# Mixture of experts: from 128-row blocks shared by two experts in split arithmetic to 64 rows for each expert in plain fp32

## The chip, the cores and the metric

The kernel runs on one core of a Trainium2 chip. The metric is the device time of one execution in microseconds (us); the median of 3 runs of the kernel before is 3462.05 us (3460.3 to 3463.83). A core has five engines with instruction queues of their own: TensorE (PE; its weight loads are listed as PEld), VectorE (DVE), ScalarE (ACT), GpSimd (POOL) and SyncE (SP, which here only issues transfers), and 16 DMA engines that carry out the transfers.

## What is computed

Two transformer blocks run one after the other on 1024 tokens of 1024 values. The change concerns the last step of the second block, a mixture of 64 experts. A router picks for each token one of 8 groups and then the two best of its 8 experts. Each expert is a small gated network, and a token's two results are added with their gates:

```python
e_in_group = jnp.take_along_axis(e_logits, g_sel[:, None, None], axis=1)[:, 0]
top_p, top_j = lax.top_k(e_prob, TOP_K)                     # TOP_K = 2
gate = g_prob_of_group * top_p / jnp.sum(top_p, axis=-1, keepdims=True)
h = jax.nn.silu(xb @ w1[e]) * (xb @ w3[e])                  # xb: 1024 wide, h: 256 wide
y = h @ w2[e]                                               # 1024 wide
```

An expert has 1024x512 values in `w1` and `w3` together and 256x1024 in `w2`, 3 MB in fp32. All 64 experts are 192 MB, and every one of them is read once. The 2048 rows (1024 tokens, two experts each) give an expert 32 rows on average. With the reference's own inputs the fullest experts have 75, 69 and 64 rows, and the fullest pair (b, b + 32) has 115.

## The kernel before

The program runs its stages in order: the first block, the second block's mixers, the merge (`phase_merge`, which also computes the router's scores), the routing (`phase_route`) and the experts (`phase_moe`). Only the last three are touched.

**Blocks.** Experts b and b + 32 share a block of 128 slots. `phase_route` counts each token's place within its pair and writes three tables by a matmul with one-hot rows: `idx` (which token sits in a slot), and two columns of `gate`, one for each of the two experts, of which one is zero for every slot. Both experts of a block compute on all 128 rows; the gate cancels the rows of the other. A table for slots beyond 128 (`idxo`, `gateo`, `eid`) feeds a loop at the end (`For_i`, L2073), which runs as many times as there are such blocks.

**Arithmetic.** Matmuls are done in fp32r. To keep fp32 accuracy every operand is split in a high part (`nc.scalar.copy` to an F32R tile) and a low part (`nc.vector.tensor_tensor` subtract), and three products are added: high by high, high by low, low by high. `wsplit` (L2000) does it for each piece of the weights, `xT` (L1990) for the transposed tokens, `hT` (L2022) for the hidden values.

**Weights.** A piece is 512 KB (128 partitions of 4 KB). `rawload` (L1942) issues one on SP's queue into the next of 34 slots (`NR` = 19 on the right side of the memory, of which 16 hold the merge's `mt` tiles first and 3 stage its weights, and `NL` = 15 on the left). `prefetch` (L1951) issues pieces ahead: during the merge as `mt` tiles come free, 13 more in `phase_route`, 4 more from POOL at the start of `phase_moe`. From then on SP issues a piece when the split has read an old one. `rawload`'s queue is in program order, so a load that waits holds up those behind it.

**Order in `phase_moe`.** Expert by expert (L2053): transposes of the hidden values of the last expert, `up` of this expert (8 steps of 128 rows, three products each, into one PSUM bank), `down` of the last one into `py`; after the second expert of a block `py` is copied by ACT and added to `out` by an indirect DMA on POOL's queue (`scatter`, L1973). Tokens are fetched two blocks ahead by an indirect DMA (`gather`, L1968).

Of the kernel before, what the change touches and what calls it, by code (L numbers as in the profile page):

```python
# [8 lines left out]
F32 = mybir.dt.float32  # L9
F32R = mybir.dt.float32r  # L10
# [10 lines left out]
NR, NL, NB, PF = 19, 15, 30, 2  # L21


def layout(inp):
# [34 lines left out]
    def heads(a, b):  # L59
# [32 lines left out]
                                    .reshape(64, 8, 128, 512).transpose(0, 2, 1, 3))  # L92
# [27 lines left out]
class K:  # L120
# [1515 lines left out]
    def phase_merge(self):  # L1636
# [22 lines left out]
        self.Oe = rp.tile([128, 2, 8, 32], F32, name="Oe")  # L1659
        with ExitStack() as st:  # L1660
# [45 lines left out]
            with ExitStack() as s1:  # L1706
# [15 lines left out]
                for c in range(8):  # L1722
# [3 lines left out]
                    if c >= 1:  # L1726
                        self.prefetch(PF if c > 1 else NR - 14)
# [98 lines left out]
    def phase_route(self):  # L1826
# [11 lines left out]
        self.gate = rp.tile([128, 2, 32], F32, name="gate")  # L1838
        self.gateo = rp.tile([128, 2, 16], F32, name="gateo")
        self.eid = rp.tile([128, 17], I32, name="eid")  # L1840
        self.rawL = self.pool("rawL", NL, ctx=self.ctxm)
        self.prefetch(NB - self.npre)
        with ExitStack() as st:
# [4 lines left out]
            Og = self.O.rearrange("p h c (s g) j -> p h c s (g j)", s=2)  # L1848
            C32 = [128, 8, 32]
            Ob = p.tile(C32, BF16, name="Ob")  # L1850
            V.tensor_tensor(Ob, Oe[:, 0], Oe[:, 1], op=ALU.add)
# [3 lines left out]
            Pb = p.tile([128, 9, 32], BF16, name="Pb")  # L1855
            V.memset(Pb[:, 0, :], 0.0)
            for c in range(8):
                V.tensor_tensor(Pb[:, c + 1, :], Pb[:, c, :], Ob[:, c, :], op=ALU.add)
            pr = ps.tile(C32, F32, name="prk")
            nc.tensor.matmul(pr, usb[:, 0, :], Ob, start=True, stop=False)  # L1860
            nc.tensor.matmul(pr, usb[:, 1, :], Pb[:, 0:8, :], start=False, stop=True)
            W = p.tile([128, 2, 8, 3, 32], F32, name="W")
            for h in range(2):
                for v in range(3):
                    src = Oe[:, h] if v == 0 else Og[:, h, :, v - 1]
                    nc.gpsimd.tensor_tensor(W[:, h, :, v, :], src, val[:, :, h, min(v, 1), None].to_broadcast(C32), op=ALU.mult)
            rk = p.tile([128, 2, 8], F32, name="rnk")
            for h in range(2):
                J = p.tile(C32, F32, name=f"J{h}")
                V.tensor_tensor(J, Oe[:, h], pr, op=ALU.mult)  # L1870
                V.tensor_reduce(rk[:, h], J, axis=AX.X, op=ALU.add)
            pt = ps.tile([128, 3, 32], F32, name="ptab")
            for i in range(16):
                h, c = divmod(i, 8)
                q = p.tile([128, 128], F32, name="q1h", bufs=6)
                V.tensor_scalar(q, io, rk[:, h, c:c + 1], None, op0=ALU.is_equal)
# [3 lines left out]
            pc = ps.tile([128, 32], F32, name="pcn")  # L1880
            nc.tensor.matmul(pc, usb[:, 1, :], Pb[:, 8, :], start=True, stop=True)
            nb = p.tile([128, 32], F32, name="nb")
            V.tensor_scalar(nb, pc, 128.0, None, op0=ALU.is_gt)
            for b in range(2, 8):
                V.scalar_tensor_tensor(nb, pc, 128.0 * b, nb, op0=ALU.is_gt, op1=ALU.add)
            ci = p.tile([128, 32], F32, name="ci")
            V.tensor_tensor_scan(ci, self.ones[:, 0:32], nb, 0.0, op0=ALU.mult, op1=ALU.add)
            oe = p.tile([128, 32], F32, name="oe")
            V.tensor_sub(oe, ci, nb)
            ob = p.tile([128, 2, 8], F32, name="obk")  # L1890
            for h in range(2):
                J = p.tile(C32, F32, name=f"J{h}")
                V.tensor_tensor(J, Oe[:, h], oe[:, None, :].to_broadcast(C32), op=ALU.mult)
                V.tensor_reduce(ob[:, h], J, axis=AX.X, op=ALU.add)
            fl = p.tile([128, 2, 8], F32, name="fl")
            V.tensor_scalar(fl, rk, 128.0, None, op0=ALU.is_ge)
            for b in range(2, 8):
                V.scalar_tensor_tensor(fl, rk, 128.0 * b, fl, op0=ALU.is_ge, op1=ALU.add)
            rm = p.tile([128, 2, 8], F32, name="rm")
            V.scalar_tensor_tensor(rm, fl, -128.0, rk, op0=ALU.mult, op1=ALU.add)  # L1900
            V.scalar_tensor_tensor(ob, fl, -1.0, ob, op0=ALU.add, op1=ALU.add)
            mo = p.tile([128, 2, 8], F32, name="mo")
            V.tensor_scalar(mo, fl, 0.0, None, op0=ALU.is_gt)
            K16 = [128, 8, 16]
            Wo = p.tile([128, 2, 8, 3, 16], F32, name="Wo")
            for h in range(2):
                kq = p.tile(K16, F32, name=f"kq{h}")
                V.tensor_tensor(kq, io[:, None, 0:16].to_broadcast(K16), ob[:, h, :, None].to_broadcast(K16), op=ALU.is_equal)
                for v in range(3):
# [255 lines left out]
```

## Time and profile before

| | |
|---|---|
| median of 3 runs | 3462.05 us |
| span of the profiled execution | 3462.8 us |
| busy share over the span: PE, DVE, ACT, POOL | 94%, 68%, 46%, 14% |
| expert stage: first matmul to last, us from the start | 2856.5 to about 3443.5 |
| pieces of expert weights loaded | 384 of 512 KB (64 x 6) |

The shares over the whole span say little here, since the stages have different limits. From about 2857 us on only the experts run, and the rows below are read from that stretch, and from a few places elsewhere that show the price of an operation the stage doesn't have yet. In rows of matmuls the duration of one is its latency; matmuls are pipelined, and what they cost in a stream is the distance of their starts.

### The profile page before, as it was taken

The numbers are of one execution on the slowest core, as the hardware profiler recorded it, in microseconds if no ns is written. First come the engines' busy times: TensorE is split into PE (matmuls) and PEld (weight loads), VectorE is DVE, ScalarE is ACT, GpSimd is POOL, SyncE is SP. The second block draws the span as 40 slices with busy tenths as digits, with TensorE's granted clock in tenths as the row PEclk, the third lists the DMA queues.
The fourth block names the chain that finished last, engine by engine and source line by source line (L and its number), as shares of the span: only waits on it lengthen the run. The fifth ranks groups of instructions, "written<-read, shape, count | busy, mean of one in ns | idle before, by whom it ended". The sixth has DMA issues, their size and how long they took to land.

```text
span 3462.8 us, 45772 instructions
## 1 busy us (share of the span) xinstructions
PE 3265.8 (94%) x17125; PEld 2641.3 (76%) x17125; DVE 2364.0 (68%) x3850; ACT 1583.9 (46%) x2961; POOL 495.4 (14%) x342
## 2 busy tenths in 40 slices
PE   7999979976999999999999899999999979999997
PEld 3788868864788888888787787777787767777876
DVE  5754259989666565564778713468884568999997
ACT  4332235563432222222455412267763218888886
POOL 0000034454300000000333100000002011112110
PEclk9999989997999999999999999999999979999999
DMA  6722221043211111111211123110025559999994
GB/s 223 239 72 83 88 94 50 29 141 122 79 57 55 49 49 49 46 49 46 83 41 42 49 73 100 48 40 25 13 75 171 189 207 347 370 357 356 356 349 173
DMA packets 180656, 440.32 MB, mean 127 GB/s; under 512 B 22288, under 2 KB 73888, under 8 KB 180176
## 3 DMA queue, kind: packets, MB, share of 16 engines
q1 hardware_dynamic: 138160, 383.48, 31.7%
q10 hardware_dynamic: 31936, 32.54, 2.7%
q0 software_dynamic: 10336, 21.34, 2.4%
q8 instruction: 136, 2.23, 0.3%
q14 instruction: 88, 0.72, 0.1%
HBM read 396.39 MB, written 57.67 MB: 131 GB/s over the span
## 4 chain that ended last, share of the span: by engine, by line
PE 68%; DVE 13%; DMA 8%; ACT 5%; issue 4%; POOL 1%; SPq 0%; ACTq 0%; POOLq 0%; DVEq 0%
PE pj L222 8%; PE pd L1065 6%; PE ph L2015 5%; PE pg L910 5%; PE pg L908 5%; PE pg L906 5%; PE py L2037 3%; DMA wraw<-in_w_dram 3%; PE pw L945 2%; PE pmla L1685 2%; PE po L1741 2%; DMA wa<-in_wadaT_dram 1%; DVE y L1242 1%; DMA wraw<-in_w2e_dram 1%; PE po L1578 1%
## 5 line engine op out<-in xcount | busy, mean ns | idle before, releaser
L2005 DVE TENSOR_TENSOR wel<-wraw,weh 128x1024 fp32r<-128x1024 f32 x384 | 458.5, 1222 | 40.5 <-ACT weh L2004 35.5
L2004 ACT CAST weh<-wraw 128x1024 fp32r<-128x1024 f32 x384 | 391.0, 1055 | 83.2 <-PE ph L2015 80.6
L157 ACT CAST wh<-wf 128x1024 fp32r<-128x1024 f32 x136 | 142.6, 1049 | 593.0 <-PE pg L908 186.7
L158 DVE TENSOR_TENSOR wl<-wf,wh 128x1024 fp32r<-128x1024 f32 x104 | 129.1, 1241 | 208.5 <-ACT wh L157 207.8
L906 PE MATMUL pg<-hx,wh 128*128 128x512 f32 (+1 forms) x864 | 262.9, 384 | 8.5 <-DVE xt L1254 6.4
L908 PE MATMUL pg<-hx,wh 128*128 128x512 f32 (+1 forms) x864 | 261.8, 384 | 0.0
L910 PE MATMUL pg<-hx,wl 128*128 128x512 f32 (+1 forms) x864 | 261.7, 384 | 0.0
L1034 DVE SCALAR_TENSOR_TENSOR acc<-pad,fcw,acc 128x1024 f32<-128x1024 f32 x176 | 226.0, 1284 | 21.3 <-ACT acc L1031 16.8
L2015 PE MATMUL ph<-wel,xh 128*128 128x512 f32 x512 | 207.3, 405 | 6.4 <-DVE wel L2005 4.6
L2015 PE MATMUL ph<-weh,xh 128*128 128x512 f32 x512 | 206.4, 403 | 2.1 <-ACT weh L2004 2.1
L2015 PE MATMUL ph<-weh,xl 128*128 128x512 f32 x512 | 201.0, 393 | 0.0
L906 PEld LDWEIGHTS pg<-hx,wh 128*128 128x128 f32 x864 | 161.4, 190 | 41.6 <-ACT ainh L157 6.8
L910 PEld LDWEIGHTS pg<-hx,wl 128*128 128x128 f32 x864 | 161.4, 190 | 31.8 <-DVE wl L158 0.3
L908 PEld LDWEIGHTS pg<-hx,wh 128*128 128x128 f32 x864 | 161.5, 190 | 31.5
L1070 DVE SCALAR_TENSOR_TENSOR x<-pd,mod,x 128x1024 f32<-128x1024 f32 x42 | 53.8, 1282 | 136.3 <-PE pd L1065 136.3
L222 PE MATMUL pj<-hxh,wh 128*128 128x512 f32 x448 | 144.0, 398 | 0.0
L222 PE MATMUL pj<-hxl,wh 128*128 128x512 f32 x448 | 143.0, 398 | 0.0
L222 PE MATMUL pj<-hxh,wl 128*128 128x512 f32 x448 | 140.7, 395 | 0.0
L992 POOL TENSOR_TENSOR sx<-sx,sqx 128x1024 f32<-128x1024 f32 x7 | 20.4, 2918 | 723.1 <-ACT sqx L991 723.1
L2015 PEld LDWEIGHTS ph<-wel,xh 128*128 128x128 f32 x512 | 96.7, 189 | 32.3 <-DVE wel L2005 14.9
L157 ACT CAST wdh<-wdf 128x512 fp32r<-128x512 f32 (+1 forms) x44 | 25.6, 583 | 200.8 <-PE pd L1065 189.4
L1973 POOL DMA_INDIRECT out_dram<-yt,idx x32 | 50.5, 1577 | 464.6 <-ACT hh L2028 453.3
(683 smaller groups left out, 8337.9 us busy)
## 6 DMA issues: line engine op xcount, KB each, us to landing
wraw<-in_w_dram SPq DMA_DIRECT2D x252, 512.0 KB, 11.7
wraw<-in_w2e_dram SPq DMA_DIRECT2D x128, 512.0 KB, 12.0
wa<-in_wadaT_dram SPq DMA_DIRECT2D x32, 512.0 KB, 4.3
wf<-in_wconv_dram SPq DMA_DIRECT2D x28, 512.0 KB, 3.5
wf<-in_wgate_dram SPq DMA_DIRECT2D x22, 512.0 KB, 3.4
wf<-in_wup_dram SPq DMA_DIRECT2D x22, 512.0 KB, 3.4
wdf<-in_wdown_dram SPq DMA_DIRECT2D x40, 256.0 KB, 2.7
wst<-in_wada_dram SPq DMA_DIRECT2D x16, 512.0 KB, 10.2
```

Source lines behind the costliest of these rows:

```text
L157: nc.scalar.copy(hi, x)
L158: (eng or nc.vector).tensor_tensor(lo, x, hi.bitcast(F32), op=ALU.subtract)
L222: nc.tensor.matmul(ps[:, o:o + n], w[:, k, :], (hl if lo else hh)[:, k, ho:ho + n], start=k == 0 and i == 0, stop=k == 7 and i == 2)
L906: nc.tensor.matmul(ps[:, o:o + n], wh[:, k, :], xh[:, k, o:o + n], start=k == 0, stop=False)
L908: nc.tensor.matmul(ps[:, o:o + n], wh[:, k, :], xl[:, k, o:o + n], start=False, stop=False)
L910: self.lastmm = nc.tensor.matmul(ps[:, o:o + n], wl[:, k, :], xh[:, k, o:o + n], start=False, stop=k == nk - 1)
L1034: nc.vector.scalar_tensor_tensor(acc, pad[:, dy:dy + 16, dx:dx + 64], cw[:, f, tp:tp + 1], acc, op0=ALU.mult, op1=ALU.add)
L1065: nc.tensor.matmul(pp[:, o:o + 512], w[:, i, :], h[:, o:o + 512], start=i == 0 and w is wh and h is a, stop=i == n - 1 and w is wl)
L2004: nc.scalar.copy(h, f)
L2005: nc.vector.tensor_tensor(l, f, h.bitcast(F32), op=ALU.subtract)
L2015: nc.tensor.matmul(ph, a[:, k, :], b[:, j, :], start=k == 0 and a is xh and b is h, stop=k == 7 and a is xl)
L2037: nc.tensor.matmul(py[:, s * 512:s * 512 + 512], a[:, j, :], b[:, s, :], start=first and j == 0 and a is hh and b is h, stop=last and j == ...
```

## The change

- An expert gets 64 slots of its own: in a block, rows 0 to 63 belong to expert b, rows 64 to 127 to expert b + 32. `phase_route` counts places for 64 experts instead of 32 pairs; `gate` has one column.
- The matmuls of a block are plain fp32 (no F32R, no splits): for each step two matmuls, one for each expert, with a stationary operand of 64 columns, writing PSUM partitions 0 to 63 and 64 to 127 of the same bank, each with the weights of its own expert as the moving operand. `wsplit` and the second halves of `xT` and `hT` go away.
- A piece of weights is 1 MB (128 partitions of 8 KB), 6 for a block; `w13` is laid out on the host to make it contiguous. There are 18 slots (9 and 9), 8 of them shared with `mt`, one staging two (before: three) of the merge's weights.
- There are 33 blocks: 32 fixed ones and one for two experts with more than 64 rows, always run, whose expert numbers SP reads from `eid` at run time. Its results are added in two indirect DMAs, one for each half. The loop at the end runs if more is left over.
- Within a block the order is `up`, the transposes of the next block's tokens, `down`. `py` is copied half by ACT and half by DVE.

The loop's body changes in the same way and is left out below, as are the other lines of `overflow`.

```diff
-NR, NL, NB, PF = 19, 15, 30, 2
+NR, NL, NX = 9, 9, 33
...
     o["w13"] = np.ascontiguousarray(np.concatenate([f["exp_w1_2"][0], f["exp_w3_2"][0]], 2)
-                                    .reshape(64, 8, 128, 512).transpose(0, 2, 1, 3))
+                                    .reshape(64, 2, 4, 128, 512).transpose(0, 1, 3, 2, 4))
...
-        def mtile():
-            return self.rawR.tile([128, 2, 512], F32, name="wraw").rearrange("p a (b f) -> p (a b) f", b=4).bitcast(F32R)
-
-        stage = [self.rawR.tile([128, 2, 512], F32, name="wraw").rearrange("p a b -> p (a b)") for i in range(NR - 16)]
-        mt = [[mtile() for j in range(2)] for c in range(8)]
+        def slot():
+            return self.rawR.tile([128, 4, 512], F32, name="wraw")
+
+        stage = [t[:, 2 * j:2 * j + 2, :].rearrange("p a b -> p (a b)") for t in [slot() for i in range(NR - 8)] for j in range(2)]
+        mt = [[t[:, 2 * j:2 * j + 2, :].rearrange("p a (b f) -> p (a b) f", b=4).bitcast(F32R) for j in range(2)]
+              for t in [slot() for c in range(8)]]
...
-                        self.prefetch(PF if c > 1 else NR - 14)
+                        self.prefetch(1 if c > 1 else NR - 7)
...
-            Ob = p.tile(C32, BF16, name="Ob")
-            V.tensor_tensor(Ob, Oe[:, 0], Oe[:, 1], op=ALU.add)
+            O = self.O.rearrange("p h c g j -> p h c (g j)")
+            C64 = [128, 8, 64]
+            Ob = p.tile(C64, BF16, name="Ob")
+            V.tensor_tensor(Ob, O[:, 0], O[:, 1], op=ALU.add)
...
+            Pb = p.tile([128, 9, 64], BF16, name="Pb")
+            V.memset(Pb[:, 0, 0:32], 0.0)
+            V.memset(Pb[:, 0, 32:64], 8.0)
...
+            self.overflow(p, ps, rk, Pb, usb, O, io)
         self.ctxt.close()
...
+    def overflow(self, p, ps, rk, Pb, usb, O, io):
+        nc, V, val = self.nc, self.nc.vector, self.val
+        pc = ps.tile([128, 64], F32, name="pcn")
+        nc.tensor.matmul(pc, usb[:, 1, :], Pb[:, 8, :], start=True, stop=True)
+        nb = p.tile([128, 64], F32, name="nb")
+        for s in range(2):
+            self.floor(nb[:, 32 * s:32 * s + 32], pc[:, 32 * s:32 * s + 32], 1.0 / 64, 0.4921875 - 16.0 * s)
...
+        for i in range(16):
+            h, c = divmod(i, 8)
+            q = p.tile([128, 128], F32, name="q1h", bufs=6)
+            V.tensor_scalar(q, io, r[:, h, c:c + 1], None, op0=ALU.is_equal)
+            nc.tensor.matmul(pto, q, Wo[:, h, c], start=i == 0, stop=i == 15)
+        ix = self.table(p, pto, self.idxo, self.gateo, 16)
+        pm = p.tile([128, 2], F32, name="pm")
...
-    def rawload(self, src, key=None, eng=None):
-        P = self.rawR if self.nraw % (NR + NL) < NR else self.rawL
+        return ix
+
+    def rawload(self, src):
+        n = self.nraw % (NR + NL)
         self.nraw += 1
-        f = P.tile([128, 2, 512], F32, name="wraw")
-        (eng or self.nc.sync).dma_start(f, src)
-        if key is not None:
-            self.pre[key] = f
+        f = (self.rawR if n < NR else self.rawL).tile([128, 4, 512], F32, name="wraw")
+        self.nc.sync.dma_start(f, src)
         return f
 
-    def prefetch(self, num, eng=None):
-        T = self.T
+    def piece(self, q, e):
+        if q < 4:
+            return self.T["w13"][e[q % 2], q // 2]
+        return self.T["w2e"][e[q % 2]].rearrange("p a (b f) -> p (a b) f", b=2)
+
+    def prefetch(self, num):
         for n in range(self.npre, self.npre + num):
-            e, q = divmod(n, 6)
-            b, h = divmod(e, 2)
-            if q < 4:
-                self.rawload(T["w13"][b + 32 * h][:, 2 * q:2 * q + 2, :], ("u", e, q), eng)
-            else:
-                self.rawload(T["w2e"][b + 32 * h][:, q - 4, :].rearrange("p (a b) -> p a b", a=2), ("d", e, q - 4), eng)
+            b, q = divmod(n, 6)
+            self.pre[b, q] = self.rawload(self.piece(q, (b, b + 32)))
         self.npre += num
...
-            e.ph = self.pool(f"psH{b}", 1, PSUM, ctx=st)
-            e.px = self.pool(f"psX{b}", b, PSUM, ctx=st)
-            e.w = self.pool(f"ew{b}", 3 if b > 1 else 2, ctx=st, side="right")
+            e.ph = self.pool(f"psH{b}", b, PSUM, ctx=st)
+            e.px = self.pool(f"psX{b}", 1, PSUM, ctx=st)
...
+        HALF = [slice(64 * s, 64 * s + 64) for s in range(2)]
...
-            return xh, xl
-
-        def wsplit(P, src, key):
-            f = self.pre.pop(key, None) or self.rawload(src)
-            h = P.w.tile([128, 2, 512], F32R, name="weh")
-            l = P.w.tile([128, 2, 512], F32R, name="wel")
-            nc.scalar.copy(h, f)
-            nc.vector.tensor_tensor(l, f, h.bitcast(F32), op=ALU.subtract)
-            return h, l
-
-        def up(P, w, xh, xl, gate, e=None):
+            t = P.t.tile([128, 8, 128], F32, name="xTt")
+            nc.scalar.copy(t, pt)
+            return t
+
...
+        def up(P, w, x, gate):
             ph = P.ph.tile([128, 512], F32, name="ph")
-            for q in range(4):
-                h, l = wsplit(P, w[:, 2 * q:2 * q + 2, :], ("u", e, q))
-                for j in range(2):
-                    k = 2 * q + j
-                    for a, b in ((xh, h), (xh, l), (xl, h)):
-                        nc.tensor.matmul(ph, a[:, k, :], b[:, j, :], start=k == 0 and a is xh and b is h,
-                                         stop=k == 7 and a is xl)
+            for q in range(2):
+                f = w(2 * q), w(2 * q + 1)
+                for j in range(4):
+                    k = 4 * q + j
+                    for s, m in enumerate(HALF):
+                        nc.tensor.matmul(ph[m], x[:, k, m], f[s][:, j, :], start=k == 0, stop=k == 7)
...
-        def hT(P, s):
+        def down(P, w, s, ix, apart=None):
...
-        def down(P, w, py, hh, hl, first, last, e=None):
+            h = P.t.tile([128, 2, 128], F32, name="hT")
+            nc.vector.tensor_copy(h, pt)
+            py = P.py.tile([128, 1024], F32, name="py")
+            f = w(4), w(5)
             for j in range(2):
-                h, l = wsplit(P, w[:, j, :].rearrange("p (a b) -> p a b", a=2), ("d", e, j))
-                for a, b in ((hh, h), (hh, l), (hl, h)):
-                    for s in range(2):
-                        nc.tensor.matmul(py[:, s * 512:s * 512 + 512], a[:, j, :], b[:, s, :],
-                                         start=first and j == 0 and a is hh and b is h,
-                                         stop=last and j == 1 and a is hl)
-
-        def store(P, py, ix):
-            y = P.t.tile([128, 1024], F32, name="yt", bufs=1)
-            nc.scalar.copy(y, py)
-            scatter(y, ix)
+                for o in range(2):
+                    for s, m in enumerate(HALF):
+                        nc.tensor.matmul(py[m, o * 512:o * 512 + 512], h[:, j, m], f[s][:, 2 * j + o, :],
+                                         start=j == 0, stop=j == 1)
+            y = P.t.tile([128, 1024], F32, name="yt")
+            nc.scalar.copy(y[:, 0:512], py[:, 0:512])
+            nc.vector.tensor_copy(y[:, 512:1024], py[:, 512:1024])
+            if apart:
+                for i in apart:
+                    scatter(y, i)
+            else:
+                scatter(y, ix)
...
-            self.prefetch(NR + NL - self.npre, nc.gpsimd)
-            X = {0: xT(P, xg[0])}
-            S, py = {}, None
-            for e in range(65):
-                b, s = divmod(e, 2)
-                if e >= 1:
-                    H = hT(P, S.pop(e - 1))
-                if s == 0 and b + 2 < 32:
-                    gather(xg[(b + 2) % NX], self.idx[:, b + 2:b + 3])
-                if s == 1 and b + 1 < 32:
-                    X[b + 1] = xT(P, xg[(b + 1) % NX])
-                if e < 64:
-                    S[e] = up(P, T["w13"][b + 32 * s], *X[b], self.gate[:, s, b:b + 1], e)
-                if e >= 1:
-                    b, s = divmod(e - 1, 2)
-                    if s == 0:
-                        py = P.py.tile([128, 1024], F32, name="py")
-                    down(P, T["w2e"][b + 32 * s], py, *H, s == 0, s == 1, e - 1)
-                    if s == 1:
-                        store(P, py, self.idx[:, b:b + 1])
-        n = nc.values_load(self.eid[0:1, 16:17], min_val=0, max_val=15)
...
+            idx = [self.idx[:, b:b + 1] for b in range(32)] + [self.idxo[:, 0:1]]
+            gate = [self.gate[:, b:b + 1] for b in range(32)] + [self.gateo[:, 0:1]]
+            for b in range(2):
+                gather(xg[b], idx[b])
+            x = xT(P, xg[0])
+            for b in range(NX):
+                if b + 2 < NX:
+                    gather(xg[(b + 2) % 3], idx[b + 2])
+                if b < 32:
+                    def w(q, b=b):
+                        return self.pre.pop((b, q), None) or self.rawload(self.piece(q, (b, b + 32)))
+                else:
+                    w = dyn(ld((slice(0, 1), slice(1, 2))))
+                s = up(P, w, x, gate[b])
+                if b + 1 < NX:
+                    x = xT(P, xg[(b + 1) % 3])
+                down(P, w, s, idx[b], [self.idxs[:, h, 0:1] for h in range(2)] if b == 32 else None)
+        n = nc.values_load(self.eid[0:1, 32:33], min_val=0, max_val=15)
```

## Rows read from the trace of the kernel before

**Rows 1.** Busy time in stretches; line: stretch, its length, engines, PE clock, DMA share, GB/s.
```profile
2850.00:2875.00 25.00, 21.78 (x97) 18.56 (x97) 17.74 (x26) 15.61 (x19) 4.85 (x5) 0.76 0.86 289
3050.00:3150.00 100.00, 99.07 (x459) 79.75 (x458) 91.30 (x93) 82.77 (x100) 20.78 (x12) 1.00 1.00 360
```
**Rows 2.** Chain that ended last, two steps one block apart: start, us, what.
```profile
3152.22 5.25 PE ph L2015 x23
3170.52 5.25 PE ph L2015 x23
```
**Rows 3.** Groups by line, from 2700 us on: operation, shapes, count, busy us, mean ns.
```profile
L2005 DVE TENSOR_TENSOR wel<-wraw,weh 128x1024 fp32r<-128x1024 f32 x384 | 458.5, 1222 | 40.5 <-ACT weh L2004 35.5 <-DMA wraw<-in_w_dram 0.5 <-DMA wraw<-in_w2e_dram 0.2
L2004 ACT CAST weh<-wraw 128x1024 fp32r<-128x1024 f32 x384 | 391.0, 1055 | 83.2 <-PE ph L2015 80.6 <-DMA wraw<-in_w_dram 0.7 <-DMA wraw<-in_w2e_dram 0.4
L2019 DVE SCALAR_TENSOR_TENSOR hs<-ph,gate,hs 128x256 f32<-128x256 f32 x64 | 30.6, 478 | 0.5 <-ACT hs L2018 0.5
L2018 ACT ACTIVATE hs<-ph 128x256 f32<-128x256 f32 x64 | 24.7, 386 | 8.6 <-PE ph L2015 8.6
```
**Rows 4.** What SP's queue waited for from 2700 us on: us in total, times, longest.
```profile
SPq L1946 <- DMA wraw<-in_w_dram: 205.8, 174, 3.3
SPq L1946 <- DVE wel L2005: 112.8, 130, 2.9
```
**Rows 5.** DMA view from 3050 to 3380 us: queues and issues to landing.
```profile
q1 hardware_dynamic: 29950, 109.06, 87.7%
q0 software_dynamic: 4896, 7.85, 9.9%
wraw<-in_w_dram SPq DMA_DIRECT2D x138, 512.0 KB, 13.2
```
**Rows 6.** Pure loads early in the program: stretches as in Rows 1, and the queue from 24 to 36 us.
```profile
24.00:30.00 6.00, 3.62 (x9) 0.72 (x7) 0.97 (x1) 4.68 (x8) 4.17 (x6) 1.00 1.03 410
q1 hardware_dynamic: 1353, 4.92, 102.8%
```
**Rows 7.** Plain fp32 matmuls of 512 columns: timeline (start, us), and all of that line.
```profile
1730.11 1.88 PE L1136 MATMUL pst<-ndg,ones 128*128 128x512 f32 x4
L1136 PE MATMUL pst<-ndg,ones x4: 592/592/592, 1730.1 to 1731.4; 128*128 128x512 f32 x4
```
**Rows 8.** Timeline, fp32r: full width, then a stationary operand of 64 columns, with weight loads.
```profile
2141.59 0.61 PE L910 MATMUL pgb<-hx,wl 128*128 128x512 f32 x2
2142.05 0.62 PE L906 MATMUL pk<-hx,wkh 128*64 128x512 f32 x2
2142.50 0.62 PE L908 MATMUL pk<-hx,wkh 128*64 128x512 f32 x2
2142.28 0.36 PEld L908 LDWEIGHTS pk<-hx,wkh 128*64 128x64 f32 x2
```
**Rows 9.** Timeline, PE: 128 rows, then 64 rows, then 128; and a run of transposes.
```profile
2332.33 0.40 PE L1535 MATMUL S<-KR,QH 128*128 128x512 f32 x1
2332.66 0.50 PE L1536 MATMUL S<-KR,QL 64*128 64x512 f32 x1
2333.09 0.44 PE L1532 MATMUL S<-kh,qh 128*128 128x384 f32 x1
3059.89 0.82 PE L1993 MATMUL pxT<-cst,xg 128*128 128x128 f32 x6
```
**Rows 10.** Timeline, the start of the expert stage.
```profile
2856.52 0.80 PE L2015 MATMUL ph<-weh,xh 128*128 128x512 f32 x1 [2.13 <-ACT weh L2004]
```
**Rows 11.** Timeline, PE in the merge: its wait for the staged weights.
```profile
2706.14 0.73 PE L1741 MATMUL po<-woh,wraw 128*128 128x512 f32 x2 [1.29 <-ACT woh L157]
```
**Rows 12.** Groups by line in the routing: a width of 512 (columns as Rows 3).
```profile
L1926 DVE TENSOR_TENSOR L<-ci,rt 128x512 f32<-128x512 f32 x1 | 0.7, 679 | 0.0
```
**Rows 13.** Timeline, POOL: the last scatter; and landing of the stage's indirect transfers.
```profile
3448.16 1.55 POOL L1973 DMA_INDIRECT out_dram<-yt,idx  x1 [11.28 <-ACTq L2073]
DMA to landing us min/median/max: 4.1/9.1/10.6
```

More of the change, by code (lines that the diff above doesn't have):

```diff
@@ L1659, in phase_merge @@
         self.Oe = rp.tile([128, 2, 8, 32], F32, name="Oe")
+        self.io2 = rp.tile([128, 128], F32, name="io2")
+        nc.vector.tensor_scalar(self.io2, self.rt[:, 0:128], 64.0, 960.0, op0=ALU.is_ge, op1=ALU.mult)
+        nc.vector.tensor_add(self.io2, self.io2, self.rt[:, 0:128])
         with ExitStack() as st:
@@ L1837, in phase_route @@
         self.idxo = rp.tile([128, 16], I32, name="idxo")
-        self.gate = rp.tile([128, 2, 32], F32, name="gate")
-        self.gateo = rp.tile([128, 2, 16], F32, name="gateo")
-        self.eid = rp.tile([128, 17], I32, name="eid")
+        self.idxs = rp.tile([128, 2, 16], I32, name="idxs")
+        self.gate = rp.tile([128, 32], F32, name="gate")
+        self.gateo = rp.tile([128, 16], F32, name="gateo")
+        self.eid = rp.tile([128, 33], I32, name="eid")
         self.rawL = self.pool("rawL", NL, ctx=self.ctxm)
-        self.prefetch(NB - self.npre)
+        self.prefetch(NR + NL - self.npre)
         with ExitStack() as st:
@@ L1875, in phase_route @@
                 q = p.tile([128, 128], F32, name="q1h", bufs=6)
-                V.tensor_scalar(q, io, rk[:, h, c:c + 1], None, op0=ALU.is_equal)
+                V.tensor_scalar(q, self.io2, rk[:, h, c:c + 1], None, op0=ALU.is_equal)
                 nc.tensor.matmul(pt, q, W[:, h, c], start=i == 0, stop=i == 15)
             self.table(p, pt, self.idx, self.gate, 32)
-            pc = ps.tile([128, 32], F32, name="pcn")
-            nc.tensor.matmul(pc, usb[:, 1, :], Pb[:, 8, :], start=True, stop=True)
@@ L1882, in phase_route @@
[L1882 to L1909, printed above, removed]
-                    vo = p.tile([128, 8], F32, name=f"vo{h}{v}")
-                    V.tensor_mul(vo, val[:, :, h, min(v, 1)], mo[:, h])
-                    if v:
-                        sd = p.tile([128, 8], F32, name=f"sd{h}{v}")
-                        V.tensor_reduce(sd, Og[:, h, :, v - 1], axis=AX.X, op=ALU.add)
-                        V.tensor_mul(vo, vo, sd)
-                    V.tensor_tensor(Wo[:, h, :, v, :], kq, vo[:, :, None].to_broadcast(K16), op=ALU.mult)
@@ L1917, in phase_route @@
-            pto = ps.tile([128, 3, 16], F32, name="ptao")
-            for i in range(16):
-                h, c = divmod(i, 8)
-                q = p.tile([128, 128], F32, name="q1h", bufs=6)
-                V.tensor_scalar(q, io, rm[:, h, c:c + 1], None, op0=ALU.is_equal)
-                nc.tensor.matmul(pto, q, Wo[:, h, c], start=i == 0, stop=i == 15)
-            self.table(p, pto, self.idxo, self.gateo, 16)
-            K64 = [128, 16, 32]
-            L = p.tile(K64, F32, name="L")
-            V.tensor_tensor(L, ci[:, None, :].to_broadcast(K64), io[:, 0:16, None].to_broadcast(K64), op=ALU.is_le)
@@ L1934, in table @@
     def table(self, p, pt, idx, gate, n):
         nc = self.nc
-        nc.scalar.copy(gate, pt[:, 1:3])
+        nc.scalar.copy(gate, pt[:, 1])
         ix = p.tile([128, n], F32, name=f"ix{n}")
@@ L1964, in phase_moe @@
         out = T["out"]
[L1965 removed]
+        xg = self.xg
         def gather(x, ix):
@@ L2046, in phase_moe, with ld @@
+        def ld(i):
+            return [nc.values_load(self.eid[0:1, j], engines=[mybir.EngineType.SP], min_val=0, max_val=63) for j in i]
         with ExitStack() as st:
             P = pools(st, 2)
[L2048 to L2069 removed]
```

109 lines of the change are left out of this document (70 added, 39 removed).

## The prediction

> **What bounds the kernel now.** I read the stretches first. In the expert stage PE is busy 99.07 of 100 us at full clock, DVE 91.30, ACT 82.77, and the DMA engines show a share of 1.00 at 360 GB/s [rows 1]. Which of these sets the pace? The chain of waits repeats every 3170.52 - 3152.22 = 18.30 us, and its steps are matmuls [rows 2], so PE sets it. The sum agrees: 72 fp32r matmuls a block at 0.228 us [rows 8] are 16.4 us, 12 transposes at (0.82 - 0.27)/5 = 0.11 us [rows 9] are 1.3 us (0.27 is one transpose's latency, an estimate from the row's length). But the transfers are hardly slower. SP waited 205.8 us for its own earlier loads and 112.8 us for DVE to free a slot [rows 4]: it holds about 8 loads open, as 13.2 us to landing times the rate, 109.06 MB in 330 us = 330 GB/s, is 4.4 MB, 8.3 loads [rows 5]. A block's 6.29 MB at 330 GB/s take 19.1 us, more than PE's 18.3. The stage runs on the stock loaded before it; **PE and the loads are bounds within 5% of each other**. What the change can win is therefore not what it takes from PE, ACT and DVE, but what the loads leave.
>
> **What goes away.** The splits, 384 on DVE at 1222 ns and 384 on ACT at 1055 ns [rows 3], beside PE's work. DVE and ACT fall to some 2 us a block (copies, Silu, gate product), so neither can be late next. 48 of 72 large matmuls of a block go too.
>
> **What PE gets.** A block has 16 matmuls up and 8 down, plain fp32. The two plain fp32 matmuls of L1136 show as four records, (1.88 - 0.592)/3 = 0.43 us apart [rows 7]; so one matmul of 512 columns is 0.86 us. A 64-column stationary operand saves nothing by itself: starts are 0.45 us apart for two, like full width [rows 8]. So a pair (two experts, one step) costs between 0.86 us, if the two halves of the array run at once, and 1.72 us, if they run in turn. Nothing in this trace shows two column halves at once. I take 0.86: the outputs lie on disjoint partitions, and the moving operand is no obstacle, as fp32r streams 512 columns in 0.228 us [rows 8], so two fp32 streams of 0.43 us a record together ask for about what one fp32r stream already gets. To this come 10 transposes (1.1 us), two changes between whole and halved array (between a 64-row and a 128-row matmul (0.33 - 0.23) + (0.43 - 0.23) = 0.3 us there and back [rows 9], the nearest row), and a stall: Silu 0.386 and gate 0.478 [rows 3] with about 0.3 us to start are mostly under the 0.88 us of the next block's transposes, then the copy of the hidden values, about 0.4 as Silu, and 0.3 to start: 1.0 us open. **PE block: 12 x 0.86 + 2.4 = 12.7 us overlapped, 12 x 1.72 + 2.4 = 23.0 us in turn.**
>
> The Trainium skill, TensorE: Matmul & The Clock Gate, section Part 3: Packing small matmuls, says that column tiles do run at once, with 2.38 measured for three tiles of 32 columns. No run here shows it. An estimate from that page: 2.38/3 = 0.79 of the ideal, 1.72/(2 x 0.79) = 1.09 us for a pair, 15.5 us a block, still under the loads.
>
> **What the loads get.** 33 x 6 = 198 pieces of 1.0486 MB, 18 of them ahead; 180 remain, 188.7 MB (before: 350 of 0.524 MB, 183.5 MB). The overflow block's gather and scatters carry few rows. Rate: at the low end 330 GB/s, as now in this stage [rows 5]; at the high end the 410 GB/s of pure loads early on [rows 6] less the 9.9% that queue 0 takes for gathers and scatters [rows 5], 369 GB/s. I take **345**, near the stage's own row. The upward step rests on two rows: the share is 0.877 + 0.099 = 0.976 in the stage but 1.03 for pure loads [rows 5, 6], so the window of 8 open loads leaves something, and it doubles in bytes. A block then needs 6.29/0.345 = 18.2 us, more than PE's 12.7: the loads are next. The new wait, PE's for two pieces at a time (one of each expert), holds up the next block's transposes and `down` behind it; with the loads as the bound that costs nothing but the last piece's 3.4 us, counted below.
>
> **Start.** First matmul at 2856.5 now, behind the first split [rows 10]; without it 1.0 us (a cast) earlier. Routing over 64 experts makes four operations on the path 512 wide, 0.68 us each [rows 12]: between 0 and 2.7 us more, I take 1.3, about half, since they exist at 256. One staging tile fewer in the merge: PE waits 1.29 us there now [rows 11]; 0 to 3 us, I take 1. First matmul about 2858. The overflow arithmetic follows the tables and is beside the first transposes, as now. The clock is at 0.76 in that stretch [rows 1], so the first half of `up` (8 matmuls, 4 pairs) goes at half speed, 6.9 us, and frees its two slots at about 2865. SP's loads wait for that, not for a split. From then on loads run without a gap.
>
> **End.** The last piece lands at 2865 + 188.7/0.345 = 2865 + 547 = 3412. Then 8 down matmuls (3.4), copies 0.9, a first scatter and, behind it on POOL, the second of the overflow block: 1.55 plus a landing of 4.1 to 9.1, I take 8 [rows 13]; from the last scatter's start to the end 3462.8 - 3448.2 = 14.6 [rows 13]. That is 27 us. Up to there POOL's queue holds one gather and one scatter a block, as now; the second scatter of the last block has only the end behind it. SP reads the two expert numbers ahead of the last six loads; behind it only they are queued, and 8 MB still in flight cover a few us. **Sum: 3439 us of span; the median lies 0.7 us under the span now, so 3438.**
>
> **Rivals.**
>
> 1. *The loads gain nothing.* 188.7/0.330 = 572 us instead of 547: 3463. For it: the share is close to 1 already; against: the pure stream's 410. The Trainium skill, DMA: Bandwidth & Descriptors, Specifications, gives about 358 GB/s as the HBM limit of a core; the trace's 410 GB/s [rows 6] goes past that, so I don't take it for the ceiling.
>
> 2. *The halves run in turn* (the other side: slower). PE then needs 33 x 23.0 = 759 us from 2858, 6 more for the half clock at the start, and 23.5 after its end: 3646. It decides as soon as a PE block exceeds (3462 - 2858 - 6 - 23.5)/33 = 17.4 us, a pair 1.25 us: the overlap must save at least 27%. For it: no row shows any; against: the reasons above.
>
> 3. *Weight loads come into the open.* 48 loads a block of about 0.135 us (two in 0.36 with starts 0.23 apart [rows 8]) are 6.5 us: a block of 19.2, 3521 in all. Against: with one array the loads hide entirely, starts staying 0.228 apart [rows 8]. The Trainium skill, same section Part 3, says that a weight load overlaps a running matmul only where the row group differs, and column halves share all rows; these rows contradict it for a whole array, none shows halves.
>
> 4. *The clock.* PE is busy 12.7 of 18.2 us and waits for loads; at 1.2 GHz a block is about 24.4 us, 805 us in all: 3688. Against: at half clock PE has no gaps, and the clock came back in the stretch after 2850 with PE busy 21.78 of 25 us [rows 1].
>
> 5. *It doesn't do what it says:* a third full expert turns the loop on, some 40 us a turn (loads 18, PE 13, chain). The reference's counts have two experts over 64 and one at exactly 64.
>
> **How the numbers follow.** Forecast (overlap, 338 to 369 GB/s, 3402 to 3450): 0.56. Rival 1: 0.15. Rival 2, with partial overlap under 27%: 0.20. Rival 3: 0.04. Rivals 4 and 5: 0.05. A measurement of this kernel tells 0.2%, 7 us, from no change; so faster 0.56, same 0.15 (rival 1), slower 0.29. The likeliest case's own range is 3402 to 3455; as 0.29 lies beyond, the range goes on to rival 2: 3402 to 3650.
>
> **What would show it.** Right: weight records of two column halves starting within one record's 0.43 us; PE busy near 70% and waiting for `wraw`; SP waiting for its own loads, not for slots; a period near 18.2 us. Pairs 1.72 us apart and PE full: rival 2. Loads at 330 GB/s: rival 1. PE clock at 0.5 for long: rival 4. The sum would be wrong at the tail if the two scatters don't follow each other, and in the middle if the rate of loads leaves 330 to 369.

## The result, and the profile after

The changed kernel takes 3420.56 us (median of four runs, 3419.28 to 3421.86) against 3462.94 us beside it: a ratio of 0.9874 (95% interval 0.986 to 0.9888), 42 us faster. The forecast was 24 us faster. The profiled execution has a span of 3419.6 us.

Stretches of the changed kernel, columns as in [rows 1] (stretch, length, PE, PEld, DVE, ACT, POOL, PE clock, DMA share, GB/s):
```profile
2850.00:2875.00 25.00, 22.13 (x93) 12.66 (x94) 6.32 (x28) 3.87 (x5) 1.97 (x2) 0.68 0.32 124
3050.00:3150.00 100.00, 81.60 (x341) 27.03 (x338) 9.60 (x18) 11.25 (x18) 15.73 (x12) 1.00 1.01 395
3350.00:3400.00 50.00, 39.02 (x148) 12.16 (x144) 4.67 (x9) 3.23 (x6) 4.64 (x3) 0.93 0.67 260
```
PE fell from 99 to 82 busy, DVE from 91 to 10, ACT from 83 to 11; the transfers rose from 360 to 395 GB/s. What each now waits for, from 2900 to 3320 us (us in total, times, longest), and the DMA queues of the same stretch (packets, MB, share of 16 engines):
```profile
SPq L1964 <- DMA wraw<-in_w_dram: 229.1, 95, 4.6
SPq L1964 <- DMA wraw<-in_w2e_dram: 132.2, 48, 4.3
SPq L1964 <- PE py L2039: 4.3, 5, 2.9
PE ph L2022 <- DMA wraw<-in_w_dram: 46.6, 40, 2.5
```
```profile
q1 hardware_dynamic: 21099, 153.64, 89.0%
q0 software_dynamic: 7488, 13.30, 12.4%
```
The weights' queue of the kernel before in the same stretch:
```profile
q1 hardware_dynamic: 38315, 139.51, 87.4%
```
SP waits 361 us for its own loads and 8 us for PE's slots (4.3 for `py`, 3.5 for `ph`); in the same stretch of the kernel before it waited 240 us for its own loads and 87 us for DVE's slots. So the loads are the bound now. They run at 153.64 MB / 420 us = 366 GB/s, against 139.51 / 420 = 332 before.

The block's period is read from the Silu, one a block (timeline of ACT: start, us, instruction, idle before it):
```profile
2907.72 0.39 ACT L2024 ACTIVATE hs<-ph 128x256 f32<-128x256 f32 x1 [6.28 <-PE ph L2022]
2920.24 0.39 ACT L2024 ACTIVATE hs<-ph 128x256 f32<-128x256 f32 x1 [6.28 <-PE ph L2022]
3035.12 0.39 ACT L2024 ACTIVATE hs<-ph 128x256 f32<-128x256 f32 x1 [10.00 <-PE ph L2022]
3374.23 0.38 ACT L2024 ACTIVATE hs<-ph 128x256 f32<-128x256 f32 x1 [9.38 <-PE ph L2022]
```
While the stock lasts the period is PE's own, 12.52 us. From 3035.12 to 3374.23 lie 20 blocks: 16.96 us each, or 6.29 MB / 16.96 = 371 GB/s.

Start and end of the stage, timeline of all engines:
```profile
2858.86 1.01 ACT L2012 COPY xTt<-pxT 128x1024 f32<-128x1024 f32 x1 [0.93 <-DVE idxs L1940]
2859.93 2.83 PE L2022 MATMUL ph<-wraw,xTt 128*64 128x512 f32 x6 [2.20 <-ACT xTt L2012]
2866.53 4.27 SPq L1964 DMA_DIRECT2D wraw<-in_w_dram  x4
3395.29 5.14 PE L2039 MATMUL py<-wraw,hT 128*64 128x512 f32 x14 [0.72 <-DMA wraw<-in_w2e_dram]
3402.05 1.55 POOL L1989 DMA_INDIRECT out_dram<-yt,idxs  x1 [15.67 <-DVEq L2084]
3407.20 1.55 POOL L1989 DMA_INDIRECT out_dram<-yt,idxs  x1 [3.60 <-DMA out_dram<-yt,idxs]
```
SP issues its next load at 2866.53, the last `down` is let go by its load at 3395.29, and 24.3 us later the kernel ends. Between the two lie the 180 pieces (DMA view from 2866 to 3396 us; GB/s of all queues in 40 slices of 13.25 us):
```profile
GB/s 352 363 410 399 408 395 389 405 394 413 405 382 394 396 403 403 382 386 406 394 398 397 399 409 398 401 406 403 396 396 390 377 401 394 401 397 420 405 287 93
q1 hardware_dynamic: 25920, 188.76, 86.7%
```
Over the whole of it the weights come to 188.7 MB / 528.8 us = 357 GB/s and not 366: in the last two slices the rate falls to 287 and 93. At 366 GB/s the pieces would have taken 516 us, so this drain of the last open loads costs about 13 us.

### The profile page after: what moved, and what is told of

Read it like the earlier page. It is cut to its first block, busy times and chain, and to the rows that moved or that the text cites. A ratio compares the mean times of both kernels' runs of the same rounds, so it can differ in the third digit from the quotient of the medians.

```text
span 3419.6 us, 42225 instructions
## 1 busy us (share of the span) xinstructions
PE 3138.7 (92%) x16351; PEld 2329.1 (68%) x16351; DVE 1883.0 (55%) x3406; ACT 1164.5 (34%) x2484; POOL 476.8 (14%) x339
## 5 line engine op out<-in xcount | busy, mean ns | idle before, releaser
L2022 PE MATMUL ph<-wraw,xTt 128*64 128x512 f32 x1056 | 281.6, 607 | 57.5 <-DMA wraw<-in_w_dram 53.4
L2022 PEld LDWEIGHTS ph<-wraw,xTt 128*64 128x64 f32 x1056 | 86.4, 138 | 231.1 <-issue 119.9
L2025 DVE SCALAR_TENSOR_TENSOR hs<-ph,gate,hs 128x256 f32<-128x256 f32 x32 | 15.5, 484 | 274.5 <-ACT hs L2024 274.5
L2039 PE MATMUL py<-wraw,hT 128*64 128x512 f32 x528 | 151.6, 613 | 7.7 <-issue 5.1
L2043 DVE COPY yt<-py 128x512 f32<-128x512 f32 x33 | 22.8, 692 | 190.7 <-ACT yt L2042 190.7
L2024 ACT ACTIVATE hs<-ph 128x256 f32<-128x256 f32 x33 | 12.7, 385 | 281.6 <-PE ph L2022 281.6
L158 POOL TENSOR_TENSOR wl<-wf,wh 128x1024 fp32r<-128x1024 f32 x32 | 84.3, 2636 | 137.0 <-ACT wh L157 134.2
L2039 PEld LDWEIGHTS py<-wraw,hT 128*64 128x64 f32 x528 | 42.3, 139 | 76.0 <-issue 65.4
```

Of the source, the lines that this page charges most:

```text
L158: (eng or nc.vector).tensor_tensor(lo, x, hi.bitcast(F32), op=ALU.subtract)
L2022: nc.tensor.matmul(ph[m], x[:, k, m], f[s][:, j, :], start=k == 0, stop=k == 7)
L2039: nc.tensor.matmul(py[m, o * 512:o * 512 + 512], h[:, j, m], f[s][:, 2 * j + o, :], start=j == 0, stop=j == 1)
L2043: nc.vector.tensor_copy(y[:, 512:1024], py[:, 512:1024])
```

## Experiments

Theory A: two 64-column matmuls run at once, PE drops under the loads, and the loads set the time. Open beside it: why the loads run at 366 instead of 332 GB/s (their size, the company of the splits, where rows lie, when slots come free).

### Old load size, new arithmetic

```
-        self.nc.sync.dma_start(f, src)
+        for i in range(2):
+            self.nc.sync.dma_start(f[:, 2 * i:2 * i + 2, :], src[:, 2 * i:2 * i + 2, :])
```


> The changed kernel with each 1 MB piece loaded by two transfers of 512 KB (rows of 4 KB, as in the kernel before); slots, order and compute are untouched. Theory A (the bytes that the 8 open loads hold, or their longer rows, lift the rate): the weights fall back from 367 GB/s to the 330 to 345 GB/s of the kernel before, the block period rises from 16.96 to 18.2 to 19.1 us, and the time is 3438 to 3463 us. Theory B (the rate rose because ACT and DVE no longer split, or because slots come free earlier; size does not matter): 367 GB/s and 3420 us within 4.

Measured: 3429.53 us, ratio 0.99 (0.9884 to 0.9917). Queue of the weights, 2900 to 3320 us:
```profile
q1 hardware_dynamic: 40585, 147.79, 89.4%
```
352 GB/s, between the two theories: with the new arithmetic the size of a load is worth 14 of the 34 GB/s and 9 us of the 42. The other 33 us come with the rest of the change.

### New load size, old arithmetic

In the kernel before: 17 slots of 8 KB a partition instead of 34 of 4 KB, one load for two halves that are split one after the other.
```
-        f = P.tile([128, 2, 512], F32, name="wraw")
+        f = P.tile([128, 4, 512], F32, name="wraw")
...
-                h, l = wsplit(P, w[:, 2 * q:2 * q + 2, :], ("u", e, q))
+                if q % 2 == 0:
+                    f = load(w[:, 2 * q:2 * q + 4, :], ("u", e, q // 2))
+                h, l = wsplit(P, f[:, 2 * (q % 2):2 * (q % 2) + 2, :])
```


> The kernel before, splits and all, with its weights loaded in pieces of 1 MB with rows of 8 KB into 17 slots instead of 34 of half the size. Theory A (PE sets the pace of the kernel before at 18.30 us a block, the loads are only close to it): the period stays 18.3 us, SP waits for slots and hardly for its own loads, and the time is 3450 to 3463 us. Theory C (the loads alone held the kernel before, and the new arithmetic has no part in the gain): the period falls towards 17 us and the time to 3420 to 3430 us.

Measured: 3463.6 us, ratio 0.9998 (0.9988 to 1.0007). What SP waited for and the weights' queue (2900 to 3320 us), one stretch, and two steps of the chain a block apart:
```profile
SPq L1947 <- DVE wel L2008: 286.8, 115, 3.2
SPq L1947 <- DVE hl L2034: 81.9, 22, 3.7
```
```profile
q1 hardware_dynamic: 19784, 144.08, 88.7%
```
```profile
3050.00:3150.00 100.00, 99.06 (x459) 79.71 (x458) 91.64 (x93) 82.64 (x99) 20.77 (x12) 1.00 1.01 375
```
```profile
3068.50 2.74 PE py L2043 x12
3086.79 2.74 PE py L2043 x12
```
The period stays 18.29 us and SP waits for slots alone: PE set the pace of the kernel before, and better loads by themselves bring no time. They run at 144.08 MB / 420 us = 343 GB/s, which is what PE asks for (6.29 MB / 18.29 us = 344). Theory A holds, C falls. Note the DMA share of 1.01 in a stage where no load waits for another.

### Neighbours from the same half

```
-                for j in range(4):
-                    k = 4 * q + j
-                    for s, m in enumerate(HALF):
+                for s, m in enumerate(HALF):
+                    for j in range(4):
+                        k = 4 * q + j
```
and the same in `down`.

> The changed kernel with the two loops swapped, so that the matmuls of one expert of a piece come in a row and then those of the other: the same instructions, but two neighbours mostly use the same column half. Theory A (the two halves of the array run at once only because neighbours alternate): 24 matmuls of 0.86 us a block in turn, less up to five overlaps where the expert changes, with 2.4 us around them: a PE block of 18.7 to 23.0 us, PE the bound, a time of 3500 to 3646 us. Rival (a 64-column matmul is short by itself, whoever its neighbour is): PE stays below the loads' 16.96 us and the time is 3420 us.

Measured: 3419.89 us, the time of the changed kernel. Timeline of PE where `down` of one block meets `up` of the next:
```profile
2916.73 4.10 PE L2039 MATMUL py<-wraw,hT 128*64 128x512 f32 x13 [0.56 <-issue]
2920.25 0.64 PE L2022 MATMUL ph<-wraw,xTt 128*64 128x512 f32 x1
2920.67 0.59 PE L2039 MATMUL py<-wraw,hT 128*64 128x512 f32 x1
2920.73 0.59 PE L2022 MATMUL ph<-wraw,xTt 128*64 128x512 f32 x1
2921.10 0.59 PE L2039 MATMUL py<-wraw,hT 128*64 128x512 f32 x1
```
My expectation took PE to go strictly in turn, and that is wrong: the first matmul of `up` starts at 2920.25, while records of the last `down` matmuls, which stand ahead of it in the program, start after it. A half that is free takes its next matmul past earlier ones that wait for the other. The block on stock became 14.48 us (Silu at 2900.29 and 2914.77) instead of 12.52, still under 16.96. So this run did not take the overlap away; the next does.

### No second half to go to

```
-                        nc.tensor.matmul(ph[m], x[:, k, m], f[s][:, j, :], start=k == 0, stop=k == 7)
+                        nc.tensor.matmul(ph[m if k == 0 else HALF[0]], x[:, k, m], f[s][:, j, :], start=k == 0,
+                                         stop=k == 7 and s == 1 or k == 0 and s == 1)
```
and the same for `j` in `down`.

> The changed kernel with the second expert's products sent to the first expert's column half, except for the first step of each sum (the second expert's result is left out of the output: it is added onto the first expert's rows). The number, size and order of the matmuls stay. After the swapped loops had cost nothing, this takes away the possibility to overlap, not the order. Theory A (two 64-column matmuls run at once where they sit on different halves, and PE holds several ready): 9 of 12 pairs in a block take 1.72 instead of 0.86 us, the PE block rises from 12.5 to 20.3 us, PE is the bound, the time is 3530 to 3560 us. Rival (a 64-column plain fp32 matmul costs 0.43 us on its own): no change, 3420 us.

Measured: 3549.25 us, ratio 1.0249 (1.0228 to 1.0269). Two neighbouring Silu, and a stretch:
```profile
3135.30 0.38 ACT L2025 ACTIVATE hs<-ph 128x256 f32<-128x256 f32 x1 [12.29 <-PE ph L2022]
3155.51 0.39 ACT L2025 ACTIVATE hs<-ph 128x256 f32<-128x256 f32 x1 [12.29 <-PE ph L2022]
```
```profile
3050.00:3150.00 100.00, 97.18 (x289) 34.17 (x288) 8.01 (x15) 9.91 (x15) 13.13 (x10) 1.00 0.94 340
```
20.21 us a block (20.3 expected) with the same instructions: the overlap of the halves is what makes the change a gain. Nine pairs lost it, (20.21 - 12.52) / 9 = 0.85 us each, one plain fp32 matmul. Rival 2 had the right price.

### Dead splits, with both sizes of load

```
+                        a = P.w.tile([128, 2, 512], F32R, name="weh")
+                        c = P.w.tile([128, 2, 512], F32R, name="wel")
+                        nc.scalar.copy(a, r)
+                        nc.vector.tensor_tensor(c, r, a.bitcast(F32), op=ALU.subtract)
```
for each half `r` of the up pieces.

> The changed kernel with the splits of the first weights put back as dead work: for each half of the four up pieces of a block an ACT cast and a DVE subtraction, 8 of each a block, whose results nobody reads. PE's work and the loads stay as they are; ACT comes to 11 and DVE to 11.5 us of a 17 us block. Theory D (the splits themselves slowed the loads, by their traffic to the same memory): two thirds of the splits of the kernel before bring two thirds of the loss, the weights fall from 371 to between 345 and 355 GB/s and the time rises to 3440 to 3460 us. Theory B (the splits held the loads only by keeping slots, which here have time): 371 GB/s and 3420 us within 4.

> The same dead splits on the kernel with 512 KB loads, so that the loads have the size and the company that they had in the kernel before, while PE has the new arithmetic. Theory D (traffic of the splits): the weights fall from 362 towards 330 GB/s, about 341 with two thirds of the splits, period 18.4 us, time about 3460 us. Theory B: 362 GB/s and 3430 us within 4; then the 330 GB/s of the kernel before came from when its slots were freed and not from what ran beside the loads.

Measured: 3530.17 and 3532.58 us, ratios 1.0197 and 1.02: slower than either theory had it. Waits of SP and PE from 2900 to 3380 us, and a stretch, with 1 MB loads:
```profile
SPq L1964 <- DVE wel L2026: 395.9, 86, 7.5
PE phT L2039 <- DVE hs L2033: 97.8, 20, 5.8
```
```profile
3050.00:3150.00 100.00, 71.37 (x282) 25.64 (x280) 55.27 (x55) 49.12 (x54) 12.07 (x9) 0.86 0.90 326
```
Both expectations missed, and the runs are inconclusive on the traffic: with one buffer each, ACT and DVE waited for each other, the gate product stood behind the splits and PE behind it, and the granted clock was 0.86 in this stretch. The loads waited for slots, so their rate says nothing. The next two runs ask again without a chain.

### Company without a chain

Eight ACT copies and eight DVE subtractions a block, first on the transposed rows with 512 KB loads:
```
+            for i in range(8):
...
+                nc.scalar.copy(a, x)
+                nc.vector.tensor_tensor(c, x, x, op=ALU.subtract)
```


> The kernel with 512 KB loads, given company that holds no slot and no chain: eight ACT copies and eight DVE subtractions of 128x1024 a block as dead work on the transposed rows, one by one of the size of a split, independent of each other. PE's work, loads and slots stay. Theory D (traffic of ACT and DVE slows the loads): the weights fall from 364 towards 330 GB/s, about 341 with two thirds of the splits, period about 18.4 instead of 17.3 us, time about 3460 us. Theory B (only when slots come free matters): 364 GB/s and 3430 us within 4.

then, behind the output copies of the changed kernel, on the weights in their slots (`r` for `x`):

> The changed kernel (1 MB loads) with dead work that reads the weights in their slots: behind each block's output copies eight ACT copies and eight DVE subtractions of 128x1024 from the four up pieces, independent of each other and of the products; no result is read. This differs from the run with company only in what is read (slots, not the transposed rows), and from the dead splits in that ACT and DVE don't wait for each other. Theory D2 (what slows the packets in the kernel before and under the dead splits is that ACT and DVE read the memory into which the loads write): the mean packet of the weights' queue grows from 283 ns towards the 302 ns of the kernel before with 1 MB loads, the weights fall from 367 to about 350 GB/s, the time rises to 3440 to 3450 us. Theory B (only when slots come free): 283 ns and 3420 us within 4, if SP hardly waits for DVE.

Measured: 3428.83 us beside 3429.53 without company, and 3421.51 us beside 3420.56. The weights' queue, 2900 to 3320 us, first the one, then the other:
```profile
q1 hardware_dynamic: 40515, 147.54, 89.4%
```
```profile
q1 hardware_dynamic: 21136, 153.92, 89.1%
```
351 and 366 GB/s, as without. The mean packet of the second is 0.891 x 16 x 420 us / 21136 = 283 ns, as in the changed kernel. Eight splits' worth of ACT and DVE work a block, two thirds of what the kernel before had, cost the loads nothing; D and D2 fall.

### Old place of the rows

```
-                                    .reshape(64, 2, 4, 128, 512).transpose(0, 1, 3, 2, 4))
+                                    .reshape(64, 8, 128, 512).transpose(0, 2, 1, 3))
...
```
with 512 KB loads that read from the places to match.

> The kernel with 512 KB loads and the first weights in the memory order of the kernel before (rows of 4 KB that lie 16 KB apart, instead of 8 KB apart). Theory G (where the rows lie in memory sets part of the rate): 364 GB/s fall towards 330, 18 to 19 us a block, 3450 to 3465 us. Theories B and D: 364 GB/s and 3430 us within 4.

Measured: 3430.56 us, ratio 0.9914 (0.9898 to 0.9931), 147.79 MB in the same stretch. G falls.

### No scatters

```
-            else:
+            elif ix is None:
                 scatter(y, ix)
```


> The changed kernel without the scatters of its 32 full blocks (their results are left out of the output; gathers, copies and the last two scatters stay). Theory F (queue 0's packets take engine time from the loads in proportion, as the prediction's high bound has it: 410 GB/s of pure loads less queue 0's share): half or more of the 11.8% of queue 0 comes free, the weights rise from 367 to 385 to 400 GB/s, the period falls from 16.96 to 15.7 to 16.3 us, the time to 3378 to 3400 us. Rival (the loads are held by the 8 that are open or by the memory, not by the engines' share): 367 GB/s and 3420 us within 4.

Measured: 3363.55 us, ratio 0.972 (0.9702 to 0.9738), 57 us under the changed kernel. Queues, 2900 to 3320 us:
```profile
q1 hardware_dynamic: 23207, 168.99, 97.1%
q0 software_dynamic: 3829, 6.48, 4.1%
```
The scatters' 12.4 - 4.1 = 8.3 points of share went to the weights (89.0 to 97.1), and these rose to 402 GB/s; in proportion, 402 x 89.0/97.1 = 369, near the 366 with the scatters. The mean packet stayed (0.971 x 16 x 420 us / 23207 = 281 ns, before 283): the weights got more of the engines' time, not faster packets. Theory F holds; the size was missed, as I expected 385 to 400 GB/s and 3378 to 3400 us.

### First products early, overflow block earlier

First, a place of its own for the first transposed rows:
```
+        self.xT0 = rp.tile([128, 8, 128], F32, name="xT0")
...
-            x = xT(P, xg[0])
+            x = xT(P, xg[0], self.xT0)
```
and a PSUM bank left free, so that the first products lie in none of the routing's.

> The changed kernel with the first block's transposed rows in a place of their own (4 KB that the routing's scratch does not use, and PSUM banks for the first products that it does not use), so that their copy and the first matmuls need not wait for the overflow table. First matmul at about 2852 instead of 2859.9 us, the loads go on at about 2859 instead of 2866.5. Theory A (the loads are the bound from their restart to the last landing): all 7.5 us arrive at the end, 3413 us. Rival (the start is hidden by the stock of 18 pieces): 3420 us within 2.

Measured: 3418.24 us, ratio 0.9867 (0.9851 to 0.9884), an interval that overlaps that of the changed kernel; its span is 3414.7. Timeline:
```profile
2851.62 6.02 PE L2025 MATMUL ph<-wraw,xT 128*64 128x512 f32 x14 [1.10 <-ACT xT L2015]
2857.68 10.10 SPq L1965 DMA_DIRECT2D wraw<-in_w_dram  x4
```
PE starts 8.3 us and the first load 8.9 us earlier, but the fourth only at about 2867, since the overflow table's matmuls now lie between those of the second half of `up`. Of 7.5 us, 4.9 reach the end in the profiled execution, and 2.3 in the median, which the rival's 3420 within 2 covers as well: these runs don't decide between the two.

Then with it the order of the blocks:
```
+            seq = list(range(31)) + [32, 31]
...
-            for b in range(NX):
+            for i, b in enumerate(seq):
...
```


> The changed kernel with the first transposed rows in a place of their own (as in the run before) and the overflow block put ahead of the last full block instead of behind it, so that one scatter and not two stands behind the last matmul. Theory A (tail in series: last landing, last down products, scatters): the 5.2 us between the two last scatters go as well, 3413 us by the median of the run with the early copy alone (3418), 3410 by its profiled execution (3414.7). Rival (the two scatters only move beside another wait, or the gathers behind them come late): 3418 us.

Measured: 3410.31 us (3407.29 to 3416.3), ratio 0.985 (0.9834 to 0.9867), span 3408.7; its slowest run is under the fastest of the changed kernel. The last scatters of the timeline:
```profile
3387.54 1.55 POOL L1990 DMA_INDIRECT out_dram<-yt,idxs  x1 [7.15 <-DMA out_dram<-yt,idxs]
3394.46 1.55 POOL L1990 DMA_INDIRECT out_dram<-yt,idx  x1 [5.37 <-DVEq L2088]
```
One scatter follows the last products. This version is the fastest that computes everything: 10 us under the changed kernel. By the profiled executions 6.0 of the span's 10.9 come with the order of the blocks (5.2 expected), but the first load, with the same edit at the start, lay 1.2 us earlier in this one (2856.46), and the runs of the two versions overlap: the share of the order is not settled.

## Why the prediction was right, point by point

**What bounds the kernel before:** right. With loads of twice the size and PE's work unchanged the period stayed 18.29 us and the time 3463.6.

**PE after:** right. A pair costs 0.86 us, the block 12.52 us (12.7 predicted); the run with one half shows the price of rival 2. The estimate of 1.09 us a pair from the Trainium skill (TensorE: Matmul & The Clock Gate, Part 3: Packing small matmuls) was too high for this case: two halves overlap fully here. Rival 3 fell: the weight loads of both halves hide (12.52 us, not 19.2). Rival 4 did not come about in the stage (clock 1.00 from 3050 to 3150 us), where PE's waits for loads are 2.5 us at most; with the dead splits, where its waits reach 5.8 us, the clock was 0.86. Rival 5 fell: 33 Silu ran, so the loop at the end did not.

**The loads' rate:** the mis-sized term. I took 345 GB/s, near the 330 of the old stage [rows 5], and kept 369 as the high bound. Measured: 366 from 2900 to 3320 us, 371 in the later blocks, and 357 over all 180 pieces with their drain. What was wrong is the choice "near the stage's own row": PE bound that stage, and with 1 MB loads at PE's old pace the rate was 343, what PE asked for and not what the loads can give. The high bound, pure loads less queue 0's share, had the right mechanism, as the run without scatters shows. That its 369 comes so near 366 is partly luck: queue 0 took 12.4% and not 9.9%, by which the same sum gives 410 x 0.876 = 359, and the size of the loads added 14. As the rate of all 180 pieces 369 would have been about as far off as 345 (511 us; 528.8 measured), since the sum has no drain.

**The sum:**

| | predicted | measured |
|---|---|---|
| loads go on at | 2865 | 2866.5 |
| 180 pieces | 547 us | 3395.3 - 2866.5 = 528.8 us |
| last landing to the end | 27 us | 3419.6 - 3395.3 = 24.3 us |
| span | 3439 | 3419.6 |

Of the 19.4 us, 18.2 are the loads' (31 by their rate, less 13 for the drain), 2.7 the tail's, less 1.5 at the start. In the tail the products and copies take 6.8 us (4.3 taken; the granted clock was 0.58 from 3395 to 3399), the two scatters lie 5.2 us apart (8 taken), and 12.4 us follow (14.6 taken). The median lies 1.0 us above this span, not 0.7 under it.

**The start:** nearly right in size, wrong in cause. The first matmul came at 2859.93, not 2858. The step "the overflow arithmetic is beside the first transposes" failed: the copy of the transposed rows waited for its last result, `idxs`, and the transposes were done at about 2851. Giving that copy its own place moved the first matmul to 2851.62.

**Still open:** why 512 KB loads ran at 332 GB/s in the kernel before and at 352 with the new arithmetic, although SP waited mostly for its own loads in both. ACT's and DVE's traffic at two thirds of its dose, the place of the rows and the size of the loads are out. The mean packet of the weights narrows down what is left (queue from 2900 to 3320 us, first with no second half to go to, then with the dead splits and 1 MB loads):
```profile
q1 hardware_dynamic: 17983, 130.99, 81.8%
q1 hardware_dynamic: 17891, 130.29, 78.6%
```
With 1 MB loads a packet takes 281 to 284 ns in the runs in which SP waits mostly for its own loads, and 301, 306 and 295 ns in the three in which it waits for slots: the kernel before with 1 MB loads (369 us of the 420) and the two shown (365 and 360 us). The run with no second half has no splits, and PE reads less in it (289 records in 100 us, 341 in the changed kernel), so neither is needed for the longer packets. They go with loads that wait for slots; how the one brings the other is not shown.

## What to carry to other kernels

When an edit makes the next resource the bound, don't price that resource by its rate in a stage that something else paced; take its rate where it ran alone, less the share of what runs beside it, and add the drain of its last transfers (13 us here). Two 64-column fp32 matmuls on different halves of the array cost one where neighbours alternate; four in a row on one half cost 2 us more a block, nine of twelve pairs on one half 7.7. And once the loads bind, look at what else is in their engines: here the accumulating scatters cost 57 us, more than the change won.

## What the hardware showed that I had not expected

- Matmuls of a free column half start ahead of earlier ones that wait for the other half (2920.25 before 2920.67 above). The Trainium skill, TensorE: Matmul & The Clock Gate, Part 3, has matmuls start and end strictly in program order; these rows differ, and the measurement decides.
- A DMA share of 1.0 is not a sign that the loads are the bound: it was 1.01 at 375 GB/s with SP waiting for slots alone, 1.01 at 395 with the loads as the bound, and 97.1 + 4.1 = 101% at 418 (175.73 MB of all queues in 420 us) without the scatters.
- Twice the size of a load bought 14 GB/s and 9 us where the loads were the bound, and no time where they were not. The Trainium skill, DMA: Bandwidth & Descriptors, Bandwidth, says to batch transfers to 1 MiB or more; the trace agrees in direction, with 9 us of 3430.
- Scatters move few bytes for their time: 13.30 - 6.48 = 6.8 MB took 8.3 points of share, 1.2 a MB, against 89.0/153.64 = 0.58 a MB for the weights.
